# ScalarE alone empties two kinds of PSUM banks in the stick-breaking stage of a two-block transformer kernel

## The chip, the cores and the metric

The kernel runs on one core of one Trainium2 chip. Time is device time in microseconds (us) of that core; the kernel before takes 2243.78 us, median of 3 runs (2243.15 to 2247.18).

## The reference, cut to what matters

Two blocks run one after the other on 1024 tokens of width 1024: the first with dilated attention, latent attention and a mixture of experts, the second with an "even" and an "odd" mixer. The change lies in the even mixer: its input projection, the rotary embedding of the retention queries and keys, and stick-breaking attention of 8 heads.

```python
def even_mixer(h, w_in, w_out):
    proj = jnp.einsum('bsd,de->bse', h, w_in)
    rq, rk, rv, rg, sq, sk, sv, sg = split_cols(proj, EVEN_SIZES)
    ret = retention(rotary(rq), rotary(rk), rv)          # 4 heads, chunks of 128
    ret = rms_norm(ret) * silu(rg)
    sb = stick_breaking(sq, sk, sv) * silu(sg)
    return concat([ret, sb]) @ w_out

def rotary(x):                                           # per head, halves x1, x2
    return concat([x1 * cos - x2 * sin, x1 * sin + x2 * cos])

def stick_breaking(q, k, v):                             # per block of 128 queries
    z = q[block] @ k[:kend].T * scale
    log_one_minus = where(strict, log_sigmoid(-z), 0.0)
    suffix = reverse_cumsum(log_one_minus) - log_one_minus
    w = where(strict, exp(log_sigmoid(z) + suffix), 0.0)
    return w @ v[:kend]
```

## The kernel before, in words

The whole program is one stream of instructions per engine; a scheduler places the instructions when the program is built, and on the chip every engine runs its own stream in order. Numbers such as L1467 are lines of the kernel before.

The stage of interest lies at 1240 to 1566 us. `stick_pair` (L1429 to L1490) treats two heads at a time, so it runs four times: pairs 0 to 3. In a pair, block i (0 to 7) holds 128 queries against 128(i+1) keys. For a block:

- `scores(i)`: TensorE writes z into banks psA (L1445); ScalarE takes two sigmoids into SBUF, sA for 1 - beta of both heads in one tile, and sB for beta, one tile per head (L91). GpSimd masks the last 128 columns of sA and sB (`strict`, L1494). VectorE runs a reversed running product over sA, a scan for each head (L1454), and multiplies it into sB (L1455): sB then holds the weights w.
- `turn(n)`, once per head: TensorE transposes sB in tiles of 128 x 128 (L1466) into a bank psB of four tiles; for i of 4 and above a second bank takes the rest. The copy to SBUF (swT, L1467) is ScalarE's for the first bank and VectorE's for the second.
- `values(i)`: TensorE multiplies swT with the values sv (L1477) into one psB bank that serves four blocks (`po`); ScalarE copies it out (L1480).

The list of steps (`steps`, L1482) is: scores(i+1), turn of both heads of i, values(i-1). `weave` puts 32 pieces of the input projection (`project`) between the steps of a pair. A pair gets two column blocks of 256: first one of the next pair's queries and keys (in pair 3: retention values), then one by rows of tokens, in 8 groups of 24 matmuls, each group of 256 columns ending in one psB bank and an evacuation:

- pair 0: values of the stick stage, `ev_v`: a ScalarE copy (L1368);
- pairs 1 and 2: `ev_rqk`, the rotation of retention's queries and keys. VectorE reads the bank three times: psB times cos (L1379), then two halves of psB, swapped, times sin (L1381), and adds the two products (L1382); the sum goes to DRAM (`rqk_d`, L1383). The tables come in by a DMA for each group (`rtab`, L1376);
- pair 3: retention values, `ev_rv`: a ScalarE copy (L1391).

All these tiles share four psB banks; `est` (the evacuation tiles of 128 x 512) has three buffers, swT four, sB three, sA one.

Of the kernel before, what the change touches and what calls it, by code (L numbers as in the profile page):

```python
# [17 lines left out]
ALU = mybir.AluOpType  # L18
# [21 lines left out]
class Kern:  # L40
# [1299 lines left out]
    def even_layer(self, combine, w, w_out, post, x_ap, emit, start, between):  # L1340

        nc, tc, I = self.nc, self.tc, self.I
        rg_d, rv_d, rqk_d = (self.dp.tile([T, 512], F32, name=n) for n in ("rg_d", "rv_d", "rqk_d"))
        with ExitStack() as es:
            left = lambda n: es.enter_context(tc.tile_pool(name=n, bufs=1, reuse_waits="tile"))
            with ExitStack() as er:
                right = lambda n: er.enter_context(tc.tile_pool(name=n, bufs=1, side="right", reuse_waits="tile"))
                hT = self.new_hT(right("hT2"))  # L1350
                wp = right("ew")
                live = {}

                def stage():
                    return wp.tile([128, 512], F32, name=self.nm("est"), tag="est", bufs=3)

                def ev_qk(ps, m, h):

                    if h == 0:
                        live["qk"[m]] = [live["sp"].tile([128, T], F32R, name=self.nm("sqk" + s), tag=f"sqk{m}{s}", bufs=2)  # L1360
                                         for s in "hl"]
                    self.split(*(t[:, h * 512:(h + 1) * 512] for t in live["qk"[m]]), ps, g=None if m else 0.125)

                def ev_v(n):
                    def ev(ps, i):
                        if i == 0:
                            live["v", n] = live["sp"].tile([128, NT, 256], F32, name=self.nm("sv"), tag="sv", bufs=2)
                        nc.scalar.copy(live["v", n][:, i], ps)  # L1368
                    return ev

                def ev_rqk(n):
                    c = slice(256 * n, 256 * n + 256)

                    def ev(ps, i):
                        tb = wp.tile([128, 2, 256], F32, name=self.nm("rtab"), tag="rtab", bufs=2)
                        nc.sync.dma_start(tb, I["ret_tab"][i * 128:(i + 1) * 128, :, c])  # L1376
                        t, u = stage()[:, :256], stage()[:, :256]
                        v4 = lambda x: x.rearrange("p (h s d) -> p h s d", s=2, d=32)
                        nc.vector.tensor_tensor(t, ps, tb[:, 0], ALU.mult)  # L1379
                        for s in range(2):  # L1380
                            nc.vector.tensor_tensor(v4(u)[:, :, s], v4(ps)[:, :, 1 - s], v4(tb[:, 1])[:, :, s], ALU.mult)  # L1381
                        nc.vector.tensor_tensor(t, t, u, ALU.add)  # L1382
                        nc.sync.dma_start(rqk_d[i * 128:(i + 1) * 128, c], t)  # L1383
                    return ev

                def ev_rv(n):
                    c = slice(256 * n, 256 * n + 256)

                    def ev(ps, i):
                        t = stage()[:, :256]  # L1390
                        nc.scalar.copy(t, ps)  # L1391
                        nc.sync.dma_start(rv_d[i * 128:(i + 1) * 128, c], t)
                    return ev

                def ev_sg(n):
                    def ev(ps, m, h):
                        t = stage()
                        self.silu(t, ps)
                        o = sbT[h][:, 2 * n + m]
                        nc.vector.tensor_tensor(o, o, t, ALU.mult)  # L1400
                    return ev

                qk = (False, ev_qk)
                proj = self.project(wp, w, hT, [qk, (True, ev_v(0)), qk, (True, ev_v(1)), qk, (True, ev_rqk(0)),
                                                qk, (True, ev_rqk(1)), (True, ev_rv(0)), (True, ev_rv(1)),
                                                (False, ev_sg(0)), (False, ev_sg(1))], 512)
                combine(hT, rg_d)
                eb = left("sbo")
                sbT = [eb.tile([128, 4, 512], F32, name=self.nm("sbT")) for _ in range(2)]
                with tc.tile_pool(name="sb", bufs=1, side="right", reuse_waits="tile") as sp:  # L1410
                    live["sp"] = sp
                    for _ in range(16):
                        next(proj)
                    for _ in range(16):
                        next(proj)
                    for p in range(4):
                        self.weave(self.stick_pair(sp, live.pop("q"), live.pop("k"), live["v", p // 2], p, sbT), proj, 32)
                W0, wsteps = self.out_weights(left("wo"), w_out, 0)
                stages, take = self.retention(left("ret"), rqk_d, rv_d, rg_d)
                main = [lambda: next(proj) for _ in range(31)]  # L1420
                pro = [st for i in range(2) for st in stages(i)]
                fill = wsteps[:2] + pro[:3] + wsteps[2:] + pro[3:]
                self.weave(main, (st() for st in fill), len(fill))
                for _ in proj:
                    pass
            self.out_proj2(W0, w_out, lambda i: sbT[i // 4][:, :, i % 4 * 128:(i % 4 + 1) * 128], stages, take, post, x_ap, emit,
                           start(), lambda: (es.close(), between()))

    def stick_pair(self, sp, q, k, sv, p, sbT):  # L1429

        nc = self.nc
# [26 lines left out]
        def turn(n):  # L1458
            i = n // 2
            B = live[n]  # L1460
            t = sp.tile([128, NT, 128], F32, name=self.nm("swT"), tag="swT", bufs=4)
            for c in range(0, i + 1, 4):
                m = min(4, i + 1 - c)
                pt = self.psB()
                for j in range(m):
                    nc.tensor.transpose(pt[:, j * 128:(j + 1) * 128], B[:, (c + j) * 128:(c + j + 1) * 128], self.ident)  # L1466
                (nc.scalar.copy if c == 0 else nc.vector.tensor_copy)(t[:, c:c + m].rearrange("p a b -> p (a b)"), pt[:, :m * 128])  # L1467
            live[n] = t

        def values(i):  # L1470
# [11 lines left out]
        def steps(i):  # L1482
            if i + 1 < NT:
                yield lambda: scores(i + 1)
            if 0 <= i < NT:
                yield lambda: turn(2 * i)
                yield lambda: turn(2 * i + 1)
            if i >= 1:
                yield lambda: values(i - 1)
# [730 lines left out]
```

## Time and profile before

| | us |
|---|---|
| median of 3 runs | 2243.78 (2243.15 to 2247.18) |
| the profiled execution, its own time | 2249.22 |
| its span in the trace | 2247.5 |
| TensorE matmuls busy | 2091.9 (93%) |
| VectorE busy | 1357.6 (60%) |
| ScalarE busy | 994.4 (44%) |
| GpSimd busy | 409.7 (18%) |

The span is what the trace covers; 1.7 us lie around it. PE is TensorE's matmuls, PEld its weight loads, DVE VectorE, ACT ScalarE, POOL GpSimd, SP the engine that issues most DMAs. Matmuls overlap, and a busy PE is not one at its peak. The mean granted TensorE clock of the execution was 0.962 of full speed.

### The profile page before, as it was taken

To read this page: it belongs to the slowest core of one execution; us is meant where nothing else is said; L and a number is where in the kernel's file an instruction comes from. 1 tells how busy PE (TensorE), PEld (TensorE's weight loads), DVE (VectorE), ACT (ScalarE), POOL (GpSimd) and SP (SyncE) were. 2 spreads that over 40 slices of the span, in tenths; PEclk is the share of its full clock that TensorE was granted. 3 is DMA by queue.
4 is the path that set the end of the run, shared out by engine and by line. 5 is a ranking of instruction groups with operands and counts; after the bars stand their busy time and mean duration, and the time that the engine had idled before them with its cause. 6 is when DMAs were issued, how large, how long until landed. Compare 5 with 4: busy or idle time off the path is not lost. (4 is left out here: it accounts for less than half of the span.)

```text
span 2247.5 us, 34156 instructions
## 1 busy us (share of the span) xinstructions
PE 2091.9 (93%) x13377; PEld 1750.7 (78%) x13377; DVE 1357.6 (60%) x2339; ACT 994.4 (44%) x1834; POOL 409.7 (18%) x466
## 2 busy tenths in 40 slices
PE   7999988999999699999679998899999999999997
PEld 7768777788888687888568787788777878888876
DVE  4331665566664589999772556655576547365663
ACT  4221764355552278888662543434232335121231
POOL 1000434000001135222140332323011000110010
PEclk9999978999999699999889999999999999999999
DMA  4310414300007489999572102122353411110142
GB/s 164 83 38 13 111 29 139 115 1 1 20 3 282 157 323 371 404 374 373 222 269 75 38 21 77 50 67 87 125 183 117 156 47 38 38 34 24 57 141 75
DMA packets 116986, 277.91 MB, mean 124 GB/s; under 512 B 15807, under 2 KB 64847, under 8 KB 104111
## 3 DMA queue, kind: packets, MB, share of 16 engines
q1 hardware_dynamic: 99496, 233.67, 29.8%
q0 software_dynamic: 11568, 23.17, 3.0%
q10 hardware_dynamic: 5760, 18.88, 2.2%
q8 instruction: 106, 1.74, 0.3%
q14 instruction: 56, 0.46, 0.1%
HBM read 236.16 MB, written 57.33 MB: 131 GB/s over the span
## 5 line engine op out<-in xcount | busy, mean ns | idle before, releaser
L106 PE MATMUL psB<-hTh,wlo 128*128 128x512 f32 (+1 forms) x640 | 262.4, 410 | 1.0 <-DVE ST L1913 1.0
L108 PE MATMUL psB<-hTh,whi 128*128 128x512 f32 (+1 forms) x640 | 252.3, 394 | 0.0
L107 PE MATMUL psB<-hTl,whi 128*128 128x512 f32 (+1 forms) x640 | 251.9, 394 | 0.0
L106 PE MATMUL psB<-whi,hTl 128*128 128x256 f32 x768 | 226.9, 295 | 10.0 <-DVE swT L1467 9.9
L107 PE MATMUL psB<-wlo,hTh 128*128 128x256 f32 x768 | 217.9, 284 | 1.7 <-DVE wlo L116 1.7
L108 PE MATMUL psB<-whi,hTh 128*128 128x256 f32 x768 | 217.8, 284 | 0.0
L106 PEld LDWEIGHTS psB<-whi,hTl 128*128 128x128 f32 x768 | 147.4, 192 | 20.6 <-DVE swT L1467 11.0
L116 DVE TENSOR_TENSOR wlo<-wraw,whi 128x512 fp32r<-128x512 f32 (+2 forms) x112 | 84.7, 761 | 129.1 <-ACT whi L115 127.4
L116 DVE TENSOR_TENSOR wgl<-wgr,wgh 128x1024 fp32r<-128x1024 f32 x132 | 155.5, 1219 | 3.7 <-ACT wgh L115 0.6
L107 PEld LDWEIGHTS psB<-wlo,hTh 128*128 128x128 f32 x768 | 147.6, 192 | 2.2 <-DVE wlo L116 1.9
L108 PEld LDWEIGHTS psB<-whi,hTh 128*128 128x128 f32 x768 | 147.3, 192 | 0.0
L106 PEld LDWEIGHTS psB<-hTh,wlo 128*128 128x128 f32 (+1 forms) x640 | 120.1, 188 | 33.6 <-issue 4.5
L108 PEld LDWEIGHTS psB<-hTh,whi 128*128 128x128 f32 (+1 forms) x640 | 119.8, 187 | 28.1
L107 PEld LDWEIGHTS psB<-hTl,whi 128*128 128x128 f32 (+1 forms) x640 | 120.1, 188 | 24.6 <-issue 1.0
L115 ACT CAST wgh<-wgr 128x1024 fp32r<-128x1024 f32 x132 | 133.1, 1068 | 0.0
L115 ACT CAST whi<-wraw 128x512 fp32r<-128x512 f32 (+2 forms) x112 | 75.8, 678 | 106.9 <-PE psB L108 58.0
L1454 DVE TENSOR_TENSOR_SCAN sA<-sA,zero 128x127 f32<-128x127 f32 (+7 forms) x64 | 86.9, 1395 | 58.7 <-POOL sA L1494 58.6
L106 PE MATMUL psB<-wgh,xTl 128*128 128x512 f32 x264 | 106.8, 404 | 1.3 <-DVE xTl L116 1.3
L825 DVE TENSOR_REDUCE nm<-psA 128x1 f32<-128x1024 f32 x64 | 78.2, 1223 | 46.2 <-PE psA L108 45.9
L108 PE MATMUL psB<-wgh,xTh 128*128 128x512 f32 x264 | 104.0, 394 | 0.0
L107 PE MATMUL psB<-wgl,xTh 128*128 128x512 f32 x264 | 103.9, 394 | 0.0
L442 POOL DMA_INDIRECT obuf<-oe,stab x33 | 62.5, 1895 | 123.2 <-ACT oe L441 112.0
(542 smaller groups left out, 5073.7 us busy)
## 6 DMA issues: line engine op xcount, KB each, us to landing
wgr<-in_w_moe SPq DMA_DIRECT2D x99, 1024.0 KB
wraw<-in_even_in SPq DMA_DIRECT2D x48, 256.0 KB
wraw<-in_odd_in SPq DMA_DIRECT2D x48, 256.0 KB
x<-in_x SPq DMA_DIRECT2D x16, 512.0 KB
x_d<-x ACTq DMA_DIRECT2D x16, 512.0 KB
oc<-obuf SPq DMA_DIRECT2D x16, 512.0 KB
xo<-x_d SPq DMA_DIRECT2D x16, 512.0 KB
wraw<-in_w_in SPq DMA_DIRECT2D x14, 512.0 KB
```

What stands on the lines that cost most here:

```text
L106: mm(ps, l[1], r[0], start=start, stop=False)
L107: mm(ps, l[0], r[1], start=False, stop=False)
L108: mm(ps, l[0], r[0], start=False, stop=stop)
L115: self.hi = nc.scalar.copy(hi, src)
L116: return lo.tensor_tensor(lo_t, src, hi.bitcast(F32), ALU.subtract)
L442: return nc.gpsimd.indirect_dma_start(out=obuf[:, :], out_offset=bass.IndirectOffsetOnAxis(ap=ri, axis=0), in_=o, in_offset=None, bounds_c ...
L825: nc.vector.tensor_reduce(nm, ps, AX.X, ALU.max, negate=True)
L1454: nc.vector.tensor_tensor_scan(r, r, self.zero_row(W - 1), 1.0, ALU.mult, ALU.add)
```

## The change

Two edits. In `turn` the second bank is copied by ScalarE too. In `ev_rqk` ScalarE first copies the bank into an `est` tile (v), and VectorE's four operations read that tile; t and u now share one `est` tile, so that a group still takes two tiles of the three.

```diff
@@ ev_rqk
-                        t, u = stage()[:, :256], stage()[:, :256]
+
+                        tu = stage()
+                        t, u = tu[:, :256], tu[:, 256:]
+                        v = stage()[:, :256]
+                        nc.scalar.copy(v, ps)
                         v4 = lambda x: x.rearrange("p (h s d) -> p h s d", s=2, d=32)
-                        nc.vector.tensor_tensor(t, ps, tb[:, 0], ALU.mult)
+                        nc.vector.tensor_tensor(t, v, tb[:, 0], ALU.mult)
                         for s in range(2):
-                            nc.vector.tensor_tensor(v4(u)[:, :, s], v4(ps)[:, :, 1 - s], v4(tb[:, 1])[:, :, s], ALU.mult)
+                            nc.vector.tensor_tensor(v4(u)[:, :, s], v4(v)[:, :, 1 - s], v4(tb[:, 1])[:, :, s], ALU.mult)
                         nc.vector.tensor_tensor(t, t, u, ALU.add)
@@ turn
-                (nc.scalar.copy if c == 0 else nc.vector.tensor_copy)(t[:, c:c + m].rearrange("p a b -> p (a b)"), pt[:, :m * 128])
+                nc.scalar.copy(t[:, c:c + m].rearrange("p a b -> p (a b)"), pt[:, :m * 128])
```

The streams of the engines move with it; lines after the first edit carry numbers higher by 4. Three places, all in pair 1 around the transposes of block 4. Names end in a buffer's number.

VectorE before, from the last product of block 5: the copies of the small second banks (swT) and the rotation (est, rtab) of two groups.

```order
L1455 TENSOR_TENSOR sB_12810<-sB_12810,sA_12808 128x767
L1467 COPY swT_12856<-psB_12863 128x128
L1379 TENSOR_TENSOR est_12880<-psB_12843,rtab_12878 128x256
L1381 TENSOR_TENSOR est_12881<-psB_12843,rtab_12878 128x4x32 x2
L1467 COPY swT_12887<-psB_12894 128x128
L1382 TENSOR_TENSOR est_12880<-est_12880,est_12881 128x256
L1379 TENSOR_TENSOR est_12933<-psB_12897,rtab_12931 128x256
```

VectorE now, from the same product.

```order
L1459 TENSOR_TENSOR sB_12810<-sB_12810,sA_12808 128x767
L1383 TENSOR_TENSOR est_12880<-est_12881,rtab_12878 128x256
L1385 TENSOR_TENSOR est_12880<-est_12881,rtab_12878 128x4x32 x2
L1386 TENSOR_TENSOR est_12880<-est_12880 128x256
L1383 TENSOR_TENSOR est_12934<-est_12935,rtab_12932 128x256
```

No row of VectorE behind the products reads a psB bank any more.

ScalarE before, from the first bank of block 4's transposes to the next block's sigmoids (sA, sB; sbT is the copy of `values`).

```order
L1467 COPY swT_12856<-psB_12857 128x512
L91 ACTIVATE sB_12810<-psA_12811 128x512
L91 ACTIVATE sB_12810<-psA_12821 128x256
L1467 COPY swT_12887<-psB_12888 128x512
L1480 COPY sbT_11260<-psB_12621 128x512
L91 ACTIVATE sA_12940<-psA_12943 128x2x512
```

ScalarE now, the same stretch.

```order
L1471 COPY swT_12856<-psB_12857 128x512
L91 ACTIVATE sB_12810<-psA_12811 128x512
L91 ACTIVATE sB_12810<-psA_12821 128x256
L1471 COPY swT_12856<-psB_12863 128x128
L1381 COPY est_12881<-psB_12843 128x256
L1471 COPY swT_12888<-psB_12889 128x512
L1471 COPY swT_12888<-psB_12895 128x128
L1484 COPY sbT_11260<-psB_12621 128x512
L1381 COPY est_12935<-psB_12898 128x256
L91 ACTIVATE sA_12942<-psA_12945 128x2x512
```

Two copies of second banks and two copies for the rotation have come in, each behind the copy whose matmuls precede its own on TensorE, and nothing else has changed place.

TensorE before, behind the transposes of block 4's second head: matmuls of `values` (swT, sv), the first scores of block 6 (psA) and the next group of the projection (psB_12897).

```order
L1477 MATMUL psB_12621<-swT_12768,sv_11450 64x128
L1477 MATMUL psB_12621<-swT_12781,sv_11450 64x128
L1445 MATMUL psA_12943<-sqkh_11901,sqkl_11743 128x512 x2
L106 MATMUL psB_12897<-whi_12659,hTl_10670 128x256
L107 MATMUL psB_12897<-wlo_12660,hTh_10669 128x256
```

TensorE now, directly behind the same transposes (psB_12889 and psB_12895).

```order
L1470 MATMUL psB_12889<-ident,sB_12728 128x128 x4
L1470 MATMUL psB_12895<-ident,sB_12728 128x128
L106 MATMUL psB_12898<-whi_12659,hTl_10670 128x256
L107 MATMUL psB_12898<-wlo_12660,hTh_10669 128x256
L108 MATMUL psB_12898<-whi_12659,hTh_10669 128x256
```

The projection's group now follows the transposes at once, and `values` and the scores come later. Over the stage, TensorE's stream is now one and the same sequence of steps in pairs 0, 1 and 2; before, pairs 1 and 2 differed from pair 0 at three blocks each.

## Rows read from the trace of the kernel before

**Rows 1.** The page, chain that ended last, shares of the span by engine.
```profile
PE 32%; issue 8%; DVE 5%; POOL 2%; DMA 1%; ACT 1%; SPq 0%; another core or an unknown queue 0%; POOLq 0%; DVEq 0%; ACTq 0%
```

**Rows 2.** Busy time by stretch, pairs 0 to 3; PEclk is the granted clock.
```profile
1240.20:1317.11 76.91, 75.15 (x578) 62.33 (x578) 44.05 (x53) 37.06 (x74) 24.98 (x32) 1.00 0.11 32
1317.11:1403.21 86.10, 77.66 (x577) 63.78 (x576) 52.15 (x80) 34.39 (x67) 25.28 (x32) 0.98 0.20 59
1403.21:1488.93 85.72, 77.50 (x578) 63.88 (x578) 53.04 (x84) 34.13 (x66) 25.38 (x32) 0.98 0.20 59
1488.93:1566.00 77.07, 75.61 (x673) 68.65 (x673) 42.32 (x52) 37.32 (x77) 27.74 (x37) 1.00 0.18 56
```

**Rows 3.** Waits at 1240 to 1566 us: total, times, longest, in us.
```profile
PEld psB L106 <- DVE swT L1467: 11.0, 4, 2.8
...
PE psB L1466 <- ACT swT L1467: 5.1, 4, 1.4
...
PEld psB L1477 <- DVE swT L1467: 4.6, 2, 2.3
...
PEld psB L1466 <- DVE sB L1455: 0.5, 1, 0.5
```

**Rows 4.** Timeline of TensorE, matmuls that waited: start, length, [idle before <-releaser].
```profile
1278.01 0.66 PE L1466 MATMUL psB<-ident,sB 128*128 128x128 f32 x4 [1.26 <-ACT swT L1467]
1279.15 0.30 PE L1466 MATMUL psB<-ident,sB 128*128 128x128 f32 x1 [0.48 <-ACT sv L1368]
...
1355.21 0.66 PE L1466 MATMUL psB<-ident,sB 128*128 128x128 f32 x4 [1.29 <-ACT swT L1467]
1360.32 0.38 PE L106 MATMUL psB<-whi,hTl 128*128 128x256 f32 x1 [2.38 <-DVE swT L1467]
1374.73 1.31 PE L1477 MATMUL psB<-swT,sv 128*64 128x128 f32 x20 [2.08 <-DVE swT L1467]
1388.59 0.39 PE L106 MATMUL psB<-whi,hTl 128*128 128x256 f32 x1 [2.58 <-DVE swT L1467]
```

**Rows 5.** Timeline of VectorE around the first of these waits.
```profile
1354.79 3.51 DVE L1454 TENSOR_TENSOR_SCAN sA<-sA,zero 128x767 f32<-128x767 f32 x2 [1.56 <-POOL sA L1494]
1358.23 1.84 DVE L1455 TENSOR_TENSOR sB<-sB,sA 128x767 f32<-128x767 f32 x2
1359.99 0.28 DVE L1467 COPY swT<-psB 128x128 f32<-128x128 f32 x1
1360.19 0.41 DVE L1379 TENSOR_TENSOR est<-psB,rtab 128x256 f32<-128x256 f32 x1
```

**Rows 6.** Timeline of ScalarE in the same stretch.
```profile
1354.54 0.61 ACT L1467 COPY swT<-psB 128x512 f32<-128x512 f32 x1
1355.01 0.92 ACT L91 ACTIVATE sB<-psA 128x512 f32<-128x512 f32 x2
```

**Rows 7.** Busy time by stretch; the last three numbers are clock, DMA share, GB/s.
```profile
1361.00:1364.00 3.00, 3.00 (x16) 3.00 (x15) 0.52 (x2) 0.00 (x0) 0.00 (x0) 0.50 0.38 120
1364.00:1365.00 1.00, 1.00 (x10) 0.86 (x10) 0.01 (x1) 0.00 (x0) 0.00 (x0) 0.94 0.10 34
1446.00:1452.00 6.00, 5.96 (x35) 5.49 (x36) 2.48 (x9) 0.63 (x1) 0.00 (x0) 0.72 0.23 67
```

**Rows 8.** Groups by form, 1240 to 1566 us: busy us, mean ns of one.
```profile
L1494 POOL TENSOR_SCALAR_AFFINE_SELECT sB<-sB 128x128 f32<-128x128 f32 x64 | 83.7, 1327 | 0.2
...
L1494 POOL TENSOR_SCALAR_AFFINE_SELECT sA<-sA 128x128 f32<-128x128 f32 x64 | 18.6, 313 | 268.9 <-ACT sA L91 268.8
...
L1382 DVE TENSOR_TENSOR est<-est,est 128x256 f32<-128x256 f32 x16 | 6.7, 417 | 0.2
```

**Rows 9.** Timeline: one store of the rotation; in pair 0 a product and a group's copy.
```profile
1361.64 0.59 SPq L1383 DMA_DIRECT2D rqk_d<-est  x1
...
1281.04 1.84 DVE L1455 TENSOR_TENSOR sB<-sB,sA 128x767 f32<-128x767 f32 x2
...
1289.25 0.37 ACT L1368 COPY sv<-psB 128x256 f32<-128x256 f32 x1 [0.18 <-PE psB L108]
```

## The prediction

> **What bounds the kernel now.** I read the chain that ended last first: of its span TensorE is 32%, by far the largest engine share, VectorE 5%, ScalarE and DMA 1% each [rows 1]. So time is saved where TensorE stops, and the views after this one look for its stops in the stage that the change touches. The busy time by stretch, one row for each pair of heads, shows the stage's fault at a glance: pairs 0 and 3 take 76.91 and 77.07 us, pairs 1 and 2 take 86.10 and 85.72, and yet matmuls are busy for only some 2 us more there [rows 2]. Pairs 1 and 2 are the two with the rotation; they are 86.10 - 76.91 = 9.19 and 85.72 - 76.91 = 8.81 us longer than pair 0. ScalarE is busy for 34 us of these 86, VectorE for 52 to 53.
>
> The waits of the four pairs name the cause. TensorE's weight loads stood 11.0 us, four times, ahead of the projection (L106), and 4.6 us, twice, ahead of `values` (L1477), each time for VectorE's copy of a second bank (swT, L1467). The only other large sum is 5.1 us in four waits for ScalarE's copy of a first bank; the transposes' wait for the products is 0.5 us [rows 3]. The timeline of TensorE places them: in pair 1 at 1360.32, 1374.73 and 1388.59, with 2.38, 2.08 and 2.58 us; pair 2 has the same three again, so all six are in the pairs with a rotation. Pair 0, with as many transposes, has none of them, only 1.26 and 0.48 us of ScalarE's [rows 4].
>
> Why VectorE's small copy is late stands in its timeline: the copy of 0.28 us, whose matmuls are long done, starts at 1359.99, behind two scans (3.51 us) and two products (1.84), and the projection's matmul starts 0.05 us after its end, at 1360.32; the rotation's read of another bank begins at 1360.19, also behind the products [rows 5, 4]. ScalarE has in that time done its copy of a first bank (1354.54) and its sigmoids (to 1355.93) [rows 6]. So two of the three banks that transposes and projection share (the fourth is `po`) are held until the products end.
>
> The waits cost a second time. After the one at 1360.32, the granted clock in 1361 to 1364 us is 0.50, the lower of the two levels (1.2 of 2.4 GHz), and 0.94 in the next microsecond; in pair 2, 1446 to 1452, it is 0.72 [rows 7]. Pair 0, with its short waits, kept 1.00 [rows 2].
>
> **Removed.** (1) The six waits. By the rows of matmuls they are 2 x (2.38 + 2.08 + 2.58) = 14.1 us, by those of weight loads 11.0 + 4.6 = 15.6. I take 15.6, which counts from the last weight load. (2) The clock drops: 3.0 x (1 - 0.50) = 1.5 and 1.0 x 0.06 = 0.06 in pair 1, 6.0 x (1 - 0.72) = 1.68 in pair 2, together 3.2 us. They go if the stops go; otherwise they stay, so this term is 0 to 3.2.
>
> **Added on ScalarE.** 32 copies of second banks (four blocks of two heads in four pairs) at 0.28 to 0.61 us [rows 5, 6], and 16 copies of 128x256 at 0.37 as `sv` has it [rows 9]: at most 32 x 0.61 + 16 x 0.37 = 25 us over four pairs, beside TensorE's work, on an engine that idles for 51 us of each of the two long pairs [rows 2]. Without idle time at the right places a copy holds what follows it on ScalarE: the next first-bank copy and the next sigmoids. In the order above, each copy stands behind that whose matmuls come earlier on TensorE, so none waits for work that TensorE does after what the next instruction needs. What is left is length. Nearest is the wait of pair 0 at 1279.15, 0.48 us for ScalarE's copy of a projection bank, which pairs 1 and 2 now get as well [rows 4]: +1.0. In pairs 0 and 3 one more copy of 0.28 us can stand ahead of a first-bank copy for which TensorE waits: +0.3 in all. Bounds: the present four waits for ScalarE vanish (-5.1, [rows 3]), or each of the four gets longer by a small copy and a rotation copy (4 x (0.28 + 0.37) = +2.6). I take +1.3, the middle ground that pair 0 shows.
>
> **Removed and kept on VectorE.** It loses 32 copies; its rotation reads SBUF where it read PSUM. An addition with both inputs in SBUF takes 417 ns for 128x256 [rows 8], the multiplication out of PSUM 0.41 [rows 5]: no change taken, and none of it is on the path, because the banks are then free already.
>
> **The evacuation tiles.** A group still takes two of three. The copy v of a column reuses the tile from which the column two before was stored. In the timeline the store is issued at 1361.64; DMA share is 0.38 until 1364 and 0.10 until 1365 [rows 9, 7], so it has landed by 3.4 us after its issue at the latest. The shortest room, by pair 0's products and copies: products at 1281.04 end at 1282.88, the rotation behind them takes 0.41, twice the 0.28 that a copy of as many elements takes [rows 5], and 0.42 [rows 8], some 1.4, so 1284.3, and the copy of two columns later is due at 1289.25 [rows 9]: 5.0 us of room for 3.4. I take 0; the price if it fails is a rival below.
>
> **DMA and the other queues.** No DMA is added or moved past another on SP; the store is issued some tenths later and nobody waits for it in this stage. GpSimd's selects stay where they are.
>
> **What is late next.** The step after the waits, in pairs 1 and 2, is what pair 0 does now: TensorE has the same sequence there, 76.91 us at a clock of 1.00. That gives a second way to the sum: 9.19 + 8.81 = 18.0 us saved.
>
> **The sum.** -15.6 - 3.2 + 1.0 + 0.3 = -17.5 us, against 18.0 by pairs. The profiled execution, 2249.22 us (its span of 2247.5 and 1.7 around it), becomes 2231.7. It lies 5.4 above the median of the runs, 2243.78, so I forecast 2243.8 - 17.5 = **2226.3 us**. Behind the stage the order is the same, and the chain that ended last is 1% DMA [rows 1], so I let the saving carry through whole. About 0.2% (4.5 us: under 2239.3 or over 2248.3) is what a measurement can tell from no change.
>
> **The rivals.**
>
> *ScalarE becomes the late one.* The banks are then freed behind sigmoids instead of scans. ScalarE's present worst waits are 1.26 to 1.29 us [rows 4]; if each of the six places gets 1.3, 7.8 us come back in place of the 1.0: -15.6 - 3.2 + 7.8 + 0.3 = -10.7, so 2233; with the clock drops kept 2236. For it: ScalarE's two sigmoids of 0.92 us stand between two of its copies [rows 6]. Against: pair 0, where ScalarE already frees the projection's banks. Chance 0.12.
>
> *VectorE's rotation is held up by GpSimd.* GpSimd's selects of sB take 1327 ns where the same selects of sA, which run while VectorE waits for them, take 313 [rows 8]: one of the two holds the other off. The rotation's multiplications now have two inputs in SBUF. If each of the 16 groups lost one operation's length, 0.42 us, and the products of the next block came that much later to TensorE, 16 x 0.42 = 6.7 us come back: 2233. Against: products are waited for by 0.5 us in all [rows 3], so most of it is hidden. Chance 0.04. The Trainium skill, "SBUF — State Buffer", section "SBUF: two separate sides", states such a rule: a VectorE operation with two SBUF inputs and a GpSimd operation that reads SBUF exclude each other for the whole instruction. By that rule the rotation was free of it before and is subject to it now; the 1327 against 313 ns agree with it.
>
> *The stop only moves.* Without the six waits TensorE reaches the next transposes 2 to 3 us earlier, and stands there for VectorE's products instead, whose scans wait for GpSimd [rows 5]. Then nothing is won: 2243.8, within 0.2%. Against: pair 0 runs the same blocks in 76.91 us, and the one wait of this kind is 0.5 us [rows 3]. Chance 0.07.
>
> *Slower: ScalarE's queue waits for a store.* If the store of two columns earlier lands late, the copy v waits, and with it every first-bank copy and sigmoid behind it, which a wait of VectorE never held. Six groups of a pair reuse a tile so; I count those before the three stops of each long pair, six in all. The change loses from 17.5 / 6 = 2.9 us each, past 0.2% from (17.5 + 4.5) / 6 = 3.7. With 5.0 us of room the store would have to land over 8.7 us after its issue; at 4 us each it gives 2243.8 - 17.5 + 24 = 2250. For it: loads of weights and tables share the DMA engines. Against: their share is 0.10 to 0.38 there [rows 7]. Chance 0.04.
>
> **How the numbers follow.** The forecast has 0.73. Its own range is 2221 (the four waits for ScalarE go too: -5.1) to 2231 (+2.6 in place of +1.3, and the 3.2 of the clock stay: 2230.8). The two cases of 0.12 and 0.04 lie at 2233 to 2236, those of 0.07 and 0.04 above. I give 2221.5 to 2235.5. Faster: 0.73 + 0.12 + 0.04 = 0.89; same 0.07; slower 0.04.
>
> **What would show it.** Right: no wait of TensorE for a VectorE copy; pairs 1 and 2 at 77 to 79 us, with a granted clock of 1.00; waits for ScalarE's swT and for its copy of the rotation's bank of some 5 to 8 us in all four pairs. Wrong: waits for ScalarE of over 1 us at six places (first rival); selects or products that grew by tenths and waits of TensorE for products (second and third); ScalarE idle ahead of v, released by a DMA of rqk_d (the last). The forecast fails as a whole if pairs 1 and 2 reach 77 us and the time does not fall by about as much: then a later stage took it back.

## The result, and the profile after

The change took 2222.64 us against 2245.48 (medians of four runs each); the ratio of the runs is 0.9893, 95% interval 0.9877 to 0.9909. That is 1.1% faster, 20 to 28 us, where the forecast had 17.5; on the median that the forecast started from, 2243.78, the ratio gives 2219.8 us, 1.7 below the low end of the range. Two more measurements of the same kernel, below, gave 0.9904 and 0.9902.

The page's chain by engine, which answers to [rows 1]: "issue" went from 8% to 3% and TensorE from 32% to 37%.

```profile
PE 37%; DVE 4%; issue 3%; DMA 2%; ACT 2%; POOL 1%; SPq 0%; another core or an unknown queue 0%; POOLq 0%; DVEq 0%; ACTq 0%
```

Busy time by stretch, pairs 0 to 3, in the columns of [rows 2] (the last stretch ends here with the last matmul of `values`):

```profile
1232.45:1308.15 75.70, 74.04 (x578) 61.92 (x577) 40.66 (x45) 39.40 (x82) 24.98 (x32) 1.00 0.11 33
1308.15:1384.01 75.86, 74.26 (x578) 61.84 (x578) 48.96 (x72) 39.20 (x82) 25.28 (x32) 1.00 0.23 65
1384.01:1462.57 78.56, 75.75 (x577) 63.24 (x576) 50.09 (x76) 39.09 (x82) 25.39 (x32) 0.98 0.22 66
1462.57:1537.44 74.87, 73.32 (x662) 66.98 (x661) 38.95 (x44) 39.36 (x85) 26.73 (x34) 1.00 0.17 53
```

For pair 3 the same end in the kernel before gives:

```profile
1488.93:1564.55 75.62, 74.16 (x662) 67.20 (x661) 42.32 (x52) 36.73 (x76) 26.36 (x34) 1.00 0.17 52
```

So the stage, from the first scores of pair 0 to the end of the last `values`, fell from 324.35 to 304.99 us: pair 0 by 1.21, pair 1 by 10.24, pair 2 by 7.16, pair 3 by 0.75, together 19.36. Pairs 1 and 2 gained most, as forecast; that pairs 0 and 3 gained too was not.

The waits of the stage, which answer to [rows 3]. No wait of TensorE for a copy by VectorE is left:

```profile
PE psB L1470 <- ACT swT L1471: 6.4, 7, 1.5
PEld psB L1470 <- ACT swT L1471: 6.1, 4, 1.8
...
PEld psB L1470 <- DVE sB L1459: 2.3, 3, 1.6
ACT est L1381 <- DMA rqk_d<-est: 1.8, 1, 1.8
...
PE psB L1470 <- DVE sB L1459: 1.2, 1, 1.2
```

TensorE's timeline names the places ([rows 4] before). Pair 1 has waits of 1.21 and 0.37 us at the transposes of block 4, as pair 0 has (1.29 and 0.37 there); pair 2 has them too, and a new one at its start, for the first products:

```profile
1346.15 0.66 PE L1470 MATMUL psB<-ident,sB 128*128 128x128 f32 x4 [1.21 <-ACT swT L1471]
1347.18 0.30 PE L1470 MATMUL psB<-ident,sB 128*128 128x128 f32 x1 [0.37 <-ACT swT L1471]
...
1389.47 0.33 PE L1470 MATMUL psB<-ident,sB 128*128 128x128 f32 x1 [1.20 <-DVE sB L1459]
...
1423.22 0.66 PE L1470 MATMUL psB<-ident,sB 128*128 128x128 f32 x4 [1.24 <-ACT swT L1471]
```

ScalarE in pair 1 at the place of [rows 6]: the second bank and the rotation's bank are emptied in 0.6 us, directly behind the two sigmoids. VectorE still has its 3.51 us of scans and its products, as in [rows 5], but now it holds no bank meanwhile; the data for the rotation waits in SBUF.

```profile
1345.95 0.92 ACT L91 ACTIVATE sB<-psA 128x512 f32<-128x512 f32 x2
1346.70 0.33 ACT L1471 COPY swT<-psB 128x128 f32<-128x128 f32 x1
1346.85 0.46 ACT L1381 COPY est<-psB 128x256 f32<-128x256 f32 x1
```

```profile
1345.74 3.51 DVE L1458 TENSOR_TENSOR_SCAN sA<-sA,zero 128x767 f32<-128x767 f32 x2 [1.56 <-POOL sA L1498]
1349.17 1.84 DVE L1459 TENSOR_TENSOR sB<-sB,sA 128x767 f32<-128x767 f32 x2
1350.94 0.41 DVE L1383 TENSOR_TENSOR est<-est,rtab 128x256 f32<-128x256 f32 x1
```

One drop of the clock is left, in pair 2, behind the wait at 1423.22. It costs 2 x (1 - 0.63) + 2 x (1 - 0.52) = 1.7 us:

```profile
1424.00:1426.00 2.00, 1.75 (x8) 1.71 (x9) 2.00 (x2) 1.04 (x4) 2.00 (x2) 0.63 0.00 0
1426.00:1428.00 2.00, 2.00 (x15) 1.78 (x15) 2.00 (x3) 0.00 (x0) 0.41 (x1) 0.52 0.00 0
```

### The profile page after: what moved, and what is told of

Its sections match the earlier page's. It is cut to its first block, busy times and chain, and to the rows that moved or that the text cites. A ratio compares the mean times of both kernels' runs of the same rounds, so it can differ in the third digit from the quotient of the medians.

```text
span 2221.6 us, 34221 instructions
## 1 busy us (share of the span) xinstructions
PE 2079.9 (94%) x13377; PEld 1742.8 (78%) x13377; DVE 1343.8 (60%) x2307; ACT 1009.1 (45%) x1882; POOL 409.0 (18%) x466
```

## The experiments

Theory A: TensorE stopped because banks were held by copies queued behind VectorE's scans, and the gain beyond the forecast comes from TensorE's own order, whose cuts of `values` went. A cut is a place where the run of `values` matmuls of one block is broken by other matmuls and taken up again later. Its rivals: the surplus is chance (B); the order alone made the gain (C); VectorE's load or its reads of PSUM are dear in themselves (D). "Stage" is the stretch defined above, in the profile of each kernel; ratios are to the kernel before, with 95% intervals.

### The change again, twice

The kernel is unaltered.

> The changed kernel once more, unaltered. Theory A (what the chip saves is the six waits, the clock drops and, which the forecast left out, the cuts of values that the old order of TensorE's stream had): ratio to the kernel before 0.989 to 0.991, a stage of 303 to 307 us from the first scores of pair 0 to the last values of pair 3, against 326. Theory B (the surplus over the forecast's 17.5 us was chance in the executions): ratio 0.992, 17 to 18 us.

Ratio 0.9904 (0.9889 to 0.9919), stage 304.95 us, pairs 75.85, 75.77, 78.29 and 75.04.

> The changed kernel unaltered, for the third time, on the chip of the two above. Theory A: stage 305 us, ratio 0.990 to 0.991, 20 to 22 us. The start of the stage in the trace, 1232 to 1240 us so far though nothing ahead of it differs, shows how much of a difference between two executions is no effect of the change.

Ratio 0.9902 (0.9883 to 0.9921), stage 304.49 us. The stage repeats to half a microsecond, so pair 0 and pair 3 gained in fact. What the ratios give beyond the stage can still be chance (B). In the three profiles the stage begins at 1232.45, 1240.32 and 1232.25 us (before: 1240.20), though the streams ahead of it are the same: a scatter of 8 us between executions which is no effect of the change. The three intervals together allow 18 to 28 us; the stage's 19.4 to 19.9 lies in the two later ones and just below the first.

### TensorE's order alone

TensorE's stream alone is pinned: each of its instructions in the stage is tied to the one before it in the program, so that the scheduler can't cut `values`.

```diff
-                        self.weave(self.stick_pair(...), proj, 32)
+                        self.weave_pinned(self.stick_pair(...), proj, 32)
...
+                if i.engine == eng:
+                    if self.pe_last is not None:
+                        self.tc.add_manual_dep(i, self.pe_last.name, dep, reason="program order")
+                    self.pe_last = i
```

> The kernel before with TensorE's stream in the stage pinned to the order of its steps, which is the changed kernel's order (values whole, behind a projection piece); all copies stay on VectorE and the rotation reads PSUM. Theory A: the cuts of values are gone, some 0.6 us each, 2 to 4 to a pair, so 5 to 6 us less, but the waits for VectorE's copies stay at 14 to 16 us or grow by what had filled them: ratio 0.996 to 1.001. Theory C (the order alone made the gain, the copies are incidental): ratio 0.990 and no wait of TensorE for VectorE's copies. Theory B: 1.000 or above.

Ratio 1.0065 (1.0049 to 1.0082), about 15 us slower and outside the 0.996 to 1.001 expected, stage 339.18 us. In the trace the sequences of VectorE and ScalarE are those of the kernel before; only TensorE's differs. The waits for VectorE's copies grew from 15.6 to 20.3 us of weight loads:

```profile
PEld psB L106 <- DVE swT L1489: 15.8, 4, 4.3
...
PEld psB L1499 <- DVE swT L1489: 4.5, 2, 2.3
```

```profile
1234.93:1311.78 76.85, 74.71 (x578) 61.97 (x578) 44.05 (x53) 37.09 (x74) 25.02 (x32) 1.00 0.11 33
1311.78:1404.22 92.44, 79.65 (x577) 65.92 (x576) 52.13 (x80) 34.43 (x67) 25.30 (x32) 0.93 0.19 55
1404.22:1498.00 93.78, 80.94 (x578) 67.32 (x578) 53.11 (x84) 34.15 (x66) 25.48 (x32) 0.91 0.18 54
```

C falls. Of theory A this much holds, that the waits stay without other copies; its size did not. Without the cuts TensorE stood longer and the clock fell further (0.93 and 0.91), which suggests that the old order's cuts had filled part of the waits. Pair 0, with whole `values` and the old copies, took 76.85 us, as before the change (76.91): its order alone wins nothing there either.

### Each edit alone

The second banks alone (`turn`):

```diff
-                (nc.scalar.copy if c == 0 else nc.vector.tensor_copy)(t[:, c:c + m]...
+                nc.scalar.copy(t[:, c:c + m]...
```

> The second banks alone: ScalarE copies them, the rotation still reads PSUM on VectorE and holds its bank behind scans and products. Theory A: the waits named swT go, but those whose bank the rotation holds come back under the rotation's name; pairs 1 and 2 keep two cuts of values each more than pair 0: 78 to 82 us each, ratio 0.992 to 0.996. If the second banks were the whole cause: pairs 1 and 2 at 76 to 77 us and ratio 0.990.

Ratio 0.9906 (0.9889 to 0.9922), stage 306.80 us; the ratio is better than theory A had expected (0.992 to 0.996), and pair 1 lies under its 78 to 82 us. Pairs 1 and 2:

```profile
1315.93:1393.47 77.54, 75.83 (x577) 62.45 (x576) 48.92 (x72) 37.04 (x75) 25.27 (x32) 1.00 0.23 66
1393.47:1472.32 78.85, 77.13 (x577) 63.77 (x576) 49.87 (x76) 36.77 (x74) 25.43 (x32) 0.98 0.22 64
```

The rotation alone, on ScalarE's copy (the change without the edit above):

> The rotation alone: ScalarE empties its bank into SBUF, the second banks are still VectorE's copies. Theory A: pairs 1 and 2 become what pair 0 was before, 77 us each with two cuts of values, and the rows of VectorE's swT copies fall to below 3 us in all, since three banks are shared and only one is then held by VectorE: ratio 0.992 to 0.993, 17 to 18 us. If the second banks alone make TensorE wait: the waits for swT stay above 10 us and the ratio above 0.996.

Ratio 0.9926 (0.9913 to 0.994), as expected, stage 310.39 us; pairs 1 and 2 took 79.57 and 78.02 where 77 was expected, and the waits for VectorE's copies fell to this:

```profile
PEld psB L1470 <- DVE swT L1471: 1.3, 2, 0.7
...
PE psB L1470 <- DVE swT L1471: 0.9, 2, 0.4
```

Either edit alone removes the six waits, but for the 1.3 us above, though each leaves one kind of bank with VectorE: the stage falls by 17.6 us with the first and 14.0 with the second, by 19.4 with both. TensorE stopped when two of three banks hung behind the scans; with one it hardly did. That the waits carried the name swT did not mean that only a change to those copies could cure them.

### VectorE's order alone

All copies stay on their engines; only the scans and products of blocks 5 to 7 move behind the copies on VectorE. They are put into a function `weights`, which `scores` calls itself for blocks 0 to 4 only; `cp` is the last copy of `turn`, and `issue_after` puts what stands in its block behind that copy.

```diff
...
             live[n] = t
+            if n % 2 and 4 <= i < NT - 1:
+                with self.tc.issue_after(cp.ins):
+                    weights(i + 1)
```

> The kernel before with every copy left on its engine and the rotation still reading PSUM; only VectorE's own order changes: from block 4 on, the scans and products of the next block stand behind the second-bank copies of this one. Theory A (TensorE waits because the copy queues behind the scans, whichever engine it is on): the waits for VectorE's swT fall from 15 us to below 3, pairs 1 and 2 to 77 to 80 us, ratio 0.990 to 0.994. Theory D (VectorE's load or its reads of PSUM cost the time, and only another engine helps): the waits stay or pass to the products, ratio 0.998 or above.

Ratio 0.9928 (0.9906 to 0.995), stage 310.82 us, pairs 1 and 2 at 78.36 and 78.31. No wait of TensorE for VectorE's swT is left. In pair 0 the copies now start at 1273.40 and, when the transposes of the second head end, at 1275.88, and the scans after them:

```profile
1273.40 0.28 DVE L1474 COPY swT<-psB 128x128 f32<-128x128 f32 x1
1275.88 0.29 DVE L1474 COPY swT<-psB 128x128 f32<-128x128 f32 x1 [2.20 <-PE psB L1473]
1276.09 3.44 DVE L1461 TENSOR_TENSOR_SCAN sA<-sA,zero 128x767 f32<-128x767 f32 x2
```

So 13.5 of the 19.4 us come without moving a single copy to ScalarE, whose sequence in the trace is that of the kernel before. TensorE's order did move with the edit (in pair 0 `values` are whole now, in pairs 1 and 2 still cut), but the run on that order alone shows that it wins nothing by itself. D falls: VectorE's busy time is that of before (190.4 against 191.6 us). What it pays for the later scans stands in its waits:

```profile
PE psB L1473 <- DVE sB L1462: 4.6, 4, 1.2
PE psB L1473 <- POOL sB L1504: 4.2, 4, 1.5
```

### A cut of `values`

In the changed kernel `values` of blocks 3 and 5 are cut in two in every pair; `values(i, 0)` and `values(i, 1)` are the halves.

```diff
-                yield lambda: turn(2 * i + 1)
+                yield lambda: (turn(2 * i + 1), values(i - 1, 0) if i in (4, 6) else None)
             if i >= 1:
-                yield lambda: values(i - 1)
+                yield lambda: values(i - 1, 1 if i in (4, 6) else None)
```

> The changed kernel with values of blocks 3 and 5 cut in two in every pair, the first half directly behind the transposes, as the stream before had it in pair 0; pair 3 has one cut of its own already. Theory A: 7 more cuts at 0.5 to 0.65 us each, 3.5 to 4.6 us on the stage's 305 and no new wait, ratio to the kernel before 0.992 to 0.993. If cuts are free: stage 305 us and ratio 0.990.

Ratio 0.9902 (0.9879 to 0.9924), stage 306.60 us, so 1.6 to 2.1 us more where 3.5 to 4.6 were expected. Pairs 0 and 1:

```profile
1234.34:1310.52 76.18, 74.58 (x579) 61.92 (x578) 40.66 (x45) 39.39 (x82) 24.98 (x32) 1.00 0.11 32
1310.52:1386.97 76.45, 74.71 (x577) 61.84 (x576) 49.02 (x72) 39.20 (x82) 25.28 (x32) 1.00 0.23 67
```

Against 75.66 to 75.86 us in the three profiles of the change, two cuts cost 0.3 to 0.5 us in pair 0 and 0.6 to 0.7 in pair 1, so 0.2 to 0.35 us for one: real, but about half of the 0.5 to 0.65 us that theory A had put on it. Pairs 2 and 3 can't be used for this, since the drop of the clock went from pair 2 (76.80) to pair 3 (77.17, at 0.98).

### ScalarE's wait for a store

```diff
-                        v = stage()[:, :256]
+                        v = wp.tile([128, 256], F32, name=self.nm("esv"), tag="esv", bufs=2)
```

The rotation's copy gets two tiles of its own, used in turn (a ring). The evacuation tiles went from three to two at the same time.

> The changed kernel with the rotation's copy v in a ring of its own (2 of 128x256) and two evacuation tiles in place of three: ScalarE then never waits for a store of rqk. If the 1.7 us for which ScalarE waited for a store at the end of pair 1 makes the products of pair 2's first block late: that wait and TensorE's 1.0 to 1.2 us go, pair 2 at 76.5 to 77.5 us in place of 78.3 to 78.6, 1 to 2 us in all (ratio 0.989 to 0.990). If not: pair 2 stays at 78.3 and up, and the loads of weights and the casts behind them make it.

Ratio 0.9885 (0.9862 to 0.9908), stage 304.27 us, pair 2 at 77.79, between the two cases expected. In the changed kernel the wait stands at the end of pair 1:

```profile
1378.32 0.37 ACT L1381 COPY est<-psB 128x256 f32<-128x256 f32 x1 [1.78 <-DMA rqk_d<-est]
```

With the ring it is VectorE that waits for the store, and TensorE's wait for the first products of pair 2 fell from 0.9 to 1.2 us to 0.4:

```profile
DVE est L1383 <- DMA rqk_d<-est: 3.5, 1, 3.5
...
PE psB L1470 <- DVE sB L1459: 0.4, 1, 0.4
```

So the store's wait explains 0.5 to 0.8 us of pair 2; its dropped clock stayed.

### One copy on each engine: where it stands in the queue

Block 4's first head is copied by VectorE in both of these, the changed kernel otherwise (`vfirst` with TensorE's order pinned).

```diff
-                nc.scalar.copy(t[:, c:c + m]...
+                (nc.vector.tensor_copy if n == 8 else nc.scalar.copy)(t[:, c:c + m]...
```

> The changed kernel, TensorE's order pinned to its steps, with both banks of block 4's first head copied by VectorE, which is idle there, in place of ScalarE, which runs four sigmoids first. Theory A (a bank is late where its copy stands behind long work, here ScalarE's): the four waits of 1.2 to 1.3 us for ScalarE's swT and 0.4 behind each go, and with them the drop of the clock in pair 2: 5 to 7 us less than the changed kernel, ratio 0.987 to 0.988. Rival: the copies on VectorE push its scans back by 0.9 us and the products get late: nothing gained, ratio 0.990.

Ratio 0.9997 (0.9981 to 1.0013), stage 327.54 us, where 0.987 to 0.988 was expected: two copies to a pair gave the whole gain back. VectorE idled before its scans, but in its stream the copies stood behind them:

```profile
1272.85 3.51 DVE L1480 TENSOR_TENSOR_SCAN sA<-sA,zero 128x767 f32<-128x767 f32 x2 [1.56 <-POOL sA L1520]
1276.28 1.84 DVE L1481 TENSOR_TENSOR sB<-sB,sA 128x767 f32<-128x767 f32 x2
1278.04 0.88 DVE L1493 COPY swT<-psB 128x512 f32<-128x512 f32 x2
```

```profile
1278.78 0.58 PE L106 MATMUL psB<-whi,hTl 128*128 128x256 f32 x1 [2.89 <-DVE swT L1493]
```

```profile
PEld psB L106 <- DVE swT L1493: 13.0, 4, 3.4
```

The second form adds, behind these copies:

```diff
+            if n == 8:
+                with self.tc.issue_after(cp.ins):
+                    weights(5)
```

> The changed kernel with block 4's first head copied by VectorE, both banks, and this time the scans and products of block 5 pinned behind these copies on VectorE. Theory A (a copy's place in its queue decides, not its engine): no wait of TensorE for VectorE's swT, in contrast to vfirst, since the copies start when the transposes end and GpSimd releases the scans only 1.5 us later; the four waits of 1.2 to 1.3 us for ScalarE's swT go: stage 297 to 300 us against 305, ratio to the kernel before 0.986 to 0.988. Theory D (a copy on VectorE in this stage is dear in itself): waits for VectorE's swT of 12 us as in vfirst, stage 320 and up.

Ratio 0.9899 (0.9881 to 0.9918), stage 300.64 us, all pairs at a clock of 1.00, pair 2 at 76.29. The same copies on the same engine, ahead of the scans, which start no later for it (37.3 us behind the stage's start, 37.4 in `vfirst`):

```profile
1272.93 0.88 DVE L1478 COPY swT<-psB 128x512 f32<-128x512 f32 x2
1274.58 3.51 DVE L1465 TENSOR_TENSOR_SCAN sA<-sA,zero 128x767 f32<-128x767 f32 x2 [0.77 <-POOL sA L1508]
```

The gain fell a little short of the 5 to 8 us expected, because a wait came behind it: the next piece of the projection now waits for ScalarE's copy of a projection bank, once in each pair.

```profile
1275.54 0.39 PE L106 MATMUL psB<-whi,hTl 128*128 128x256 f32 x1 [1.11 <-ACT sv L1368]
```

Stage 300.64 against 327.54 settles the cause for theory A. TensorE was pinned in `vfirst` and not in `vfirst2`, but the traces show the same sequence of operations in both on TensorE and on ScalarE; on VectorE the only difference is that in each pair the two copies stand ahead of block 5's two scans and two products in place of behind them.

> The kernel of vfirst2 with the rotation's copy in a ring of its own as in estv. Theory A: the two gains add, 0.5 to 1 us below vfirst2 in the stage, 297 to 299 us; the ratio can't tell it from vfirst2. If the ring only helped through the drop of the clock in pair 2: the same stage as vfirst2.

The ring of `estv` and the order of `vfirst2` together: ratio 0.9876 (0.9855 to 0.9897), median 2219.73 us, stage 299.97 us, pair 2 at 75.51. The stage is 4.5 to 5 us shorter than the change's; by the medians on one chip it is 4 us better (2219.73 against 2223.84), which the intervals of the ratios don't separate.

## Where the prediction was right, and where it fell short

**The cause and the main term were right.** The six waits, 14.1 to 15.6 us, went. That they came from the copies' place behind the scans is shown by three kernels: VectorE's order alone (-13.5 us in the stage), and the same copies behind and ahead of the scans (327.5 against 300.6).

**ScalarE's load was right.** +1.3 us was forecast. Its waits at the transposes went from 5.1 us, and 0.48 for a projection bank, to 6.4: +0.8.

**The step that failed is the one called "What is late next"**, with the +0.3 us for pairs 0 and 3. It took pair 0's 76.91 us as the floor that pairs 1 and 2 reach, and let pairs 0 and 3 lose a little. But the floor moved: TensorE's stream changes in these pairs too (`values` whole where it was cut twice in pair 0), and the small second-bank copy left VectorE there as well. Pair 0 fell by 1.1 to 1.3 us, pair 3 by 0.6 to 0.8, pair 1 to 75.7 to 75.9. With 1.2 and 0.7 us for pairs 0 and 3, and a floor lower by 1.05 for pairs 1 and 2, the sum is 9.2 + 8.8 + 1.2 + 0.7 + 2 x 1.05 = 22.0 us. Four kernels divide pair 0's 1.2 us. With VectorE's copies it takes 76.91 us with cuts and 76.85 without (`order`); with ScalarE's copies 76.18 with cuts (`split`, at somewhat other places) and 75.66 to 75.85 without. So some 0.7 us come from the copies alone, and the cuts' 0.3 to 0.5 only once the banks are free in time. In pair 1 two cuts cost 0.6 to 0.7. What in the copies carries the 0.7 us no run shows.

**Two smaller steps, the other way.** Of the 3.2 us of the clock 1.7 stayed, in pair 2. Pair 2 also gained a wait for its first products, 0.9 to 1.2 us in all in the three profiles, of which the rival with the store carries 0.5 to 0.8. These 2.6 to 2.9 us bring 22.0 down to 19.1 to 19.4; measured were 19.4 to 19.9.

**The rest.** The medians and ratios give 20 to 24 us, the stage 19.4 to 19.9. Behind the stage nothing was won: from its end to the last instruction it is 2247.5 - 1564.55 = 682.95 us before and 2221.6 - 1537.44 = 684.16 after. Ahead of it the streams are the same and the start scatters by 8 us. The scatter covers the difference, but what it is was not shown. It decides where the result lies: the stage's 19.4 us alone would have given 2224.4, inside the range, and so would the two later ratios (2221.8 and 2222.2). So the stage explains 1.9 us of the surplus over 17.5. The other 4.6 us, which put the first measurement under the range, stay open and may be luck; of the kernel before there is but one profile to read the stage from.

**The low end of the range.** It was added up wrongly. The four waits for ScalarE were to go in place of the +1.3, as at the upper end; that gives 2243.8 - 15.6 - 3.2 - 5.1 = 2219.9, not 2221. The measured 2219.8 is no sign that this case came true: these waits stayed, with 6.4 us.

**The rivals.** ScalarE late at six places: TensorE's waits of over 1 us for ScalarE stand once in each pair, at block 4, as before. The rotation held up by GpSimd: on average its first multiplication takes 417 ns (0.41 us in [rows 5]) and its addition 435 (417 in [rows 8]), and the selects of sB 1334 (1327). That is hardly a test, because 58 of the 64 rotation operations run when no select does; the last section shows one that meets them. The stop that only moves: 1.2 us at one place. The store: once, 1.6 to 1.8 us, instead of six times; the room was enough for the other groups, but not for one at the end of pair 1, behind two stores that are issued 1.3 us apart:

```profile
1373.86 0.55 SPq L1387 DMA_DIRECT2D rqk_d<-est  x1
...
1375.14 0.56 SPq L1387 DMA_DIRECT2D rqk_d<-est  x1
```

## What to carry to other kernels

When TensorE waits for a short copy, look at what stands ahead of the copy in its engine's queue before asking which engine is faster: putting the copies ahead of the scans on the same engine won two thirds of what moving them to another did, and the place of the same two copies in each pair made 27 us of difference. Waits that share a pool of banks carry the name of the last one freed; freeing another member of the pool can cure them as well, so two such edits don't add. And when a stage is compared with an undisturbed twin, ask first whether the change moves the twin too.

## What was not expected of the hardware

The remaining drop of the clock chooses one of four like places. The same wait of 1.1 to 1.6 us, in three pairs with 0.4 behind it, stands at block 4 of every pair, and the granted clock fell to the lower level directly behind only one of them: in pair 2 in all three profiles of the change (and in `turn` and `estv`), in pair 3 when `values` were cut, in pair 1 with the rotation alone (0.5 behind the wait there). Where that wait was gone (`vfirst2`, `best`) the clock stayed at 1.00 in all four pairs. What singles out the one pair the rows don't show.

GpSimd's select of sB takes 0.29 us for one beside an idle VectorE and 1.68 beside its scans, both in the kernel with VectorE's order changed:

```profile
1275.21 0.29 POOL L1504 TENSOR_SCALAR_AFFINE_SELECT sB<-sB 128x128 f32<-128x128 f32 x1
1276.25 1.68 POOL L1504 TENSOR_SCALAR_AFFINE_SELECT sB<-sB 128x128 f32<-128x128 f32 x1 [0.75 <-ACT sB L91]
```

The slow one starts 0.16 us into the first of two scans, whose row is shown above (1276.09, 3.44 us for both), and lasts about until that scan ends. The Trainium skill, "SBUF — State Buffer", section "SBUF: two separate sides", has a VectorE operation with two SBUF inputs and a GpSimd operation that reads SBUF exclude each other for the whole instruction, and these rows agree. The prediction has the rotation free of this before the change; its addition was not, which had two SBUF inputs then too. Now all of it has, but mostly runs when no select does. At the start of pair 2 of the changed kernel its addition meets one: it takes 0.51 us where it takes 0.43 alone, and the two selects, the first of them beside another VectorE operation, 1.17 where two take 0.54 beside an idle VectorE:

```profile
1387.48 1.17 POOL L1498 TENSOR_SCALAR_AFFINE_SELECT sB<-sB 128x128 f32<-128x128 f32 x2
...
1387.99 0.51 DVE L1386 TENSOR_TENSOR est<-est 128x256 f32<-128x256 f32 x1
```
